# A two-branch encoder on one core: the prompt's squares summed once, more junk products at the start, sample rows in three loads, keys transposed later

## The chip, the cores and the metric

The kernel runs on one core of a Trainium2 chip. Such a core has several engines with queues of their own, each of which works its instructions off in order: TensorE (PE in the profile; PEld are its weight loads), VectorE (DVE), ScalarE (ACT), GpSimd (POOL) and SyncE (SP), which issues nearly all the DMA transfers here. They wait for each other by semaphores. The metric is the device time of one execution in microseconds (us), the median of several runs.

## The reference

Two layers over two groups of tokens, a prompt of 512 and a sample of 256, with 1024 features. In each layer the input is normalised by its root mean square, scaled and shifted by a modulation made from a condition vector, and projected; branch A is neighbourhood attention with 8 heads, branch B grouped-query attention with 8 query and 2 key heads, whose queries and keys are normalised per head and rotated.

```python
mod = jax.nn.silu(c) @ w_ada + b_ada
shift, scale, gate = jnp.split(mod, 3, axis=-1)
hid = _rms_norm(x, norm_g) * (1.0 + scale[:, None, :]) + shift[:, None, :]
proj = hid @ w_in
...
oa = _neighbourhood_attention(qa, ka, va, rpb)
ya = (oa * jax.nn.silu(za)) @ w_pa
qh = _axial_rope(_rms_norm(qb, q_norm_g))
kh = _axial_rope(_rms_norm(kb, k_norm_g))
ob = _gqa_attention(qh, kh, vb)
yb = (ob * jax.nn.silu(zb)) @ w_pb
merged = g_a * ya + g_b * yb
return x + gate[:, None, :] * (merged @ w_out)
```

(Reshapes are left out in these lines; g_a and g_b are sigmoid gates of the input.) After the two layers comes a last normalisation.

## The kernel before

**Tiles.** Activations lie with features on partitions: eight tiles per group, 128 x 512 for the prompt (`xs[0][k]`) and 128 x 256 for the sample (`xs[1][k]`; three of them share one tile in memory, `x_s`). Every operand of a projection is split into a high part and a remainder: ACT copies the high part (`whi` of the weights, `hh` of the activations, `zh`, `GK`), DVE subtracts to get the remainder (`wlo`, `hl`, `zl`), and a product takes three matmuls, high x high, high x low and low x high. In the profile the first projection is `accw<-whi,hh` and so on (512 columns), and later ones are `accp` (512 columns, the prompt) and `accs` (256 columns, the sample).

**Start.** Before the first accw stand, on TensorE: *junk* products of constants (`warm`); the modulation of the first layer, `adap` (the condition with one quarter of `wad`, four matmuls for two loads `adaraw`) and `adat` (its rows turned into columns); the sum of the prompt's squares over the features, `ssps`, by products with ones; and `rb`, which spreads the factor 1/rms over the partitions. ACT squares the eight prompt tiles as they land. `SG="PGPVPGPV"` says for each tile whether its squares are added to those of the tile before, on GpSimd (G) or DVE (V), or begin a new pair (P): four pairs, each summed by an `ssps` set of four products. `ms` and `newton` on DVE (lines 383 and 359 to 366) make the factor. Then DVE scales each x (line 276), ACT makes hh (284), DVE hl (290). The sample goes the same way later, with its seven adds of squares on GpSimd.

The order in this part is made while the program is built: each piece is a `job` with an engine, an assumed duration, what it depends on, and a rank; `run_jobs` plays them through and writes the instructions in the order of the assumed starts. Loads are put in by assumed times of a transfer, and junk products by `WARM=(10, 16.0, 0.8)`: ten at first, then one each 0.8 us of the assumed time until 16. Only the order reaches the chip; there each engine waits for what it needs.

**Later.** From then on the order follows a counter of steps. A `step` writes some six matmuls of a projection, and `defer(n, fn)` puts a piece of other work n steps behind. Attention comes in `slots`, a list that is worked off at a rate of so many per step. Branch B's keys are an example: `kv_evac` takes the key projection from PSUM in three blocks of two token tiles, and rotates it (ACT, DVE, GpSimd); `kfin`, deferred by `KF` steps, makes the per-head factor (the newton chain) and multiplies the rotated keys `rr` by it on DVE (line 1339; of the three blocks the third is deferred by one more step); `ktr`, deferred by `KT` steps, transposes them on TensorE (`kt`, line 1423, four tiles of the prompt and two of the sample), and `evac_k` copies them to `GK` on ACT (lines 676 and 677) and writes their remainders on DVE (680 and 681). All that time the projection of the gate path goes on: ACT takes tanh into `zt`, DVE multiplies (line 1447), GpSimd multiplies by the attention's output (line 1450), ACT copies `zh` (1457), DVE subtracts `zl` (1461). The scores of branch B are `gsp<-GK,GQ`; they use two buffers in PSUM, of which one comes free when ACT has taken the exponential `gp` (line 913), behind the maximum `gss` on DVE (903). `SGQ` is the number of steps before the first scores, and the rate of the slots is `len(slots)/RG`.

Of the kernel before, what the change touches and what calls it, by code (L numbers as in the profile page):

```python
# [7 lines left out]
F32 = mybir.dt.float32  # L8
# [16 lines left out]
SC = dict(  # L25

    LA=7,
    T0=3.6,
    U=0.68,

    SG="PGPVPGPV",
    WARM=(10, 16.0, 0.8),

    PW=("wor01", "wor11", "va3"),

# [6 lines left out]
    QTT=2,  # L42
    QS=6,
    QST=12,
    KF=6,
    KT=8,
    SGQ=12,
    RG=88,

    SR0=90,  # L50
    SR1=40,
# [7 lines left out]


@with_exitstack
def trunk(ctx: ExitStack, tc: tile.TileContext, xT, wst, wad, wsd, vec, gain, trig, mask, eye, rpb, yT):
    nc = tc.nc
    A, V, G, T, S = nc.scalar, nc.vector, nc.gpsimd, nc.tensor, nc.sync

# [49 lines left out]
    def mm(out, lhsT, rhs, start, stop):  # L115
        T.matmul(out=out, lhsT=lhsT, rhs=rhs, start=start, stop=stop, skip_group_check=True)  # L116
# [26 lines left out]
    def defer(k, fn):  # L143
        later.setdefault(step_no[0] + k, []).append(fn)
# [868 lines left out]
    with tc.manual_schedule():  # L1013
# [51 lines left out]

        plan = []

        def load_x(g, k):
            o, n = RNG[g]
            S.dma_start(out=xs[g][k], in_=xT[128 * k:128 * k + 128, o:o + n])  # L1070

        dma = [0.0]

        def load(units, fn):
            t = SC["T0"] + SC["U"] * dma[0]
            dma[0] += units
            plan.append((t - SC["LA"], -1, fn))
            return t + SC["U"] * units
# [58 lines left out]

# [2 lines left out]
        sq = {}  # L1140

        def square(g, k):
            sq[g, k] = galloc([128, RNG[g][1]], F32, "sq")
            A.activation(out=sq[g, k], in_=xs[g][k], func=AF.Square)

        def sq_add(g, k, base, eng):
            eng.tensor_add(out=sq[g, base], in0=sq[g, base], in1=sq[g, k])
            gfree(sq.pop((g, k)))

        def sq_sum(k, first, last):  # L1150
            if first:
                hcell["ps"] = ps_acc.tile([128, 4], F32, tag="acc", name="ssps")
            for i in range(4):
                mm(hcell["ps"][:, i:i + 1], sq[0, k][:, 128 * i:128 * i + 128], ones[:, 0:1],
                   first and i == 0, last and i == 3)
            gfree(sq.pop((0, k)))

        jsum = []
        for k in range(KC):
            j = job("ACT", 0.63, [], lambda k=k: square(0, k), 1, tx[k])  # L1160
            kind = SC["SG"][k]
            if kind in "VG":
                eng, dur = (G, 1.1) if kind == "G" else (V, 0.8)
                j = job("POOL" if kind == "G" else "DVE", dur, [jprev, j], lambda k=k, eng=eng: sq_add(0, k, k - 1, eng), 1)
            jprev, base = j, k - (kind in "VG")
            if k == KC - 1 or SC["SG"][k + 1] == "P":
                jsum.append(job("PE", 0.95, [j] + jsum[-1:],
                                lambda k=base, first=not jsum, last=k == KC - 1: sq_sum(k, first, last), 0))
        j = jsum[-1]
        for (fn,), (eng, dur) in zip(rms_chain(0, hcell)[1:], (("DVE", 2.4), ("PE", 1.0))):  # L1170
            j = job(eng, dur, [j], fn, 0)
        jrb = j
# [19 lines left out]
        for k in range(KC):  # L1192
            j = job("ACT", 0.36, [], lambda k=k: square(1, k), 12, txs[k])
            if k:
                jadd = [job("POOL", 0.6, [j] + jadd, lambda k=k: sq_add(1, k, 0, G), 12)]
            else:
                jadd = [j]

# [2 lines left out]
            sums[0][0]()  # L1201

        sums = rms_chain(1, scell)
        j = job("PE", 0.4, jadd + [jfin[0, 3], jfin[1, 3]], sample_sum, 0)
        for (fn,), (eng, dur) in zip(sums[1:], (("DVE", 2.4), ("PE", 0.5))):
            j = job(eng, dur, [j], fn, 9)
        for k in range(KC):
# [18 lines left out]
        for l in range(DEPTH):  # L1226
# [102 lines left out]
            def rope_finish(rs, ss):  # L1329

                n, nh = ss.shape[1], ss.shape[2]
                V.tensor_scalar(out=ss, in0=ss, scalar1=1.0 / 64, scalar2=EPS, op0=ALU.mult, op1=ALU.add)
                y = newton(ss.rearrange("p t h -> p (t h)"), n * nh).rearrange("p (t h) -> p t h", h=nh)
                t = 0
                for i, r in enumerate(rs):
                    k = r.shape[1]

                    def scale(r=r, k=k, t=t):
                        V.tensor_mul(out=r, in0=r, in1=y[:, t:t + k, :].unsqueeze(3).to_broadcast([128, k, nh, 64]))

                    t += k
                    if i < 2:
                        scale()
                    else:
                        defer(i // 2, scale)
# [6 lines left out]
            def q_evac(i, acc):  # L1352
                qr[i] = galloc([128, 1, 8, 64], F32, "rr")
                rope_part(acc.rearrange("p (t h d) -> p t h d", t=1, d=64), tabs[0][:, i:i + 1], qr[i], qss[:, i:i + 1, :])
                if i == 3:
                    defer(SC["QF"], lambda: rope_finish([qr[t] for t in range(4)], qss[:, 0:4, :]))
                    for pr in range(4):
                        defer(SC["QT"] + SC["QTT"] * pr, lambda pr=pr: q_tr_p(pr))
                if i == 5:
                    defer(SC["QS"], lambda: rope_finish([qr[t] for t in (4, 5)], qss[:, 4:6, :]))  # L1360
                    for w in range(2):
                        defer(SC["QST"] + SC["QTT"] * w, lambda w=w: q_tr_s(w))
# [28 lines left out]
            wide_pass(("qb", l), [(0, 1), (2,), (3,), (4, 5)], q_evac,  # L1391
                      lambda i: ps_acc.tile([128, NP], F32, tag="acc", name="accw"))
            nxt(("kvb", l))
            kr = []
            kss = smp.tile([128, 6, 2], F32, tag="qss2", name="qss", bufs=1)
            vg = vp.tile([128, 6, 4, 128], F32R, tag="v", name="vg")

            def kv_evac(b, acc):
                kr.append(galloc([128, 2, 2, 64], F32, "rr"))
                rope_part(acc[:, :, 0:128].rearrange("p t (h d) -> p t h d", d=64), tabs[1][:, 2 * b:2 * b + 2], kr[b],  # L1400
                          kss[:, 2 * b:2 * b + 2, :])
# [10 lines left out]
            roping[0] = False  # L1412

            def kfin():
                rope_finish(kr, kss)

            def ktr():
                o = [r[:, t].rearrange("p h d -> p (h d)") for r in kr for t in range(2)]
                GK.extend([[galloc([128, NT], F32R, "GK") for _ in range(2)] for _ in range(2)])
                for g, (c, n) in enumerate(RNG):  # L1420
                    t = ps_t.tile([128, n], F32, tag="t", name="kt")
                    for j in range(n // 128):
                        T.transpose(t[:, 128 * j:128 * j + 128], o[4 * g + j], ident)
                    for hp in range(2):
                        evac_k(GK[hp][0], GK[hp][1], hp, t, slice(c, c + n))
                for t_ in kr:
                    gfree(t_)
                for t_ in tabs:
                    gfree(t_)

            defer(SC["KF"], kfin)
            defer(SC["KT"], ktr)
# [268 lines left out]
def _layout(inputs):  # L1701
# [100 lines left out]
    rp = np.zeros((DEPTH, 8, RPB_LEN), dtype=f)  # L1802
    rp[:, :, 820 - 464:820 + 1] = flat[:, :, ::-1]

    arrays = dict(xT=xT, wst=wst, wad=wad, wsd=wsd, vec=vec, gain=gain, trig=trig, mask=mask, eye=np.eye(128, dtype=f), rpb=rp)
    return {k: np.ascontiguousarray(v) for k, v in arrays.items()}


_INS = ["xT", "wst", "wad", "wsd", "vec", "gain", "trig", "mask", "eye", "rpb"]


# [22 lines left out]
```

## Time and profile before

| | us |
|---|---|
| median of 3 runs | 1252.98 |
| lowest and highest | 1250.73, 1256.64 |
| profiled execution | 1254.29 |
| its span | 1252.5 |
| TensorE busy in it | 1216.3 (97%) |
| VectorE, ScalarE, GpSimd busy | 813.2, 580.9, 358.3 |
| mean granted TensorE clock | 0.984 of full |

A timeline row has the start, the time taken, engine, line, operation, output and inputs with their shapes, a count, and in brackets the idle time of the engine before it with what ended that. A matmul's own time includes its tail, so the cost of one in a dense row is the distance between two starts. In a row of the windows view the numbers are the stretch, its length, and for each engine its busy time and its instructions, then the granted clock, the DMA share and GB/s.

### The profile page before, as it was taken

The numbers are of one execution on the slowest core, as the hardware profiler recorded it, in microseconds if no ns is written. First come the engines' busy times: TensorE is split into PE (matmuls) and PEld (weight loads), VectorE is DVE, ScalarE is ACT, GpSimd is POOL, SyncE is SP. The second block draws the span as 40 slices with busy tenths as digits, with TensorE's granted clock in tenths as the row PEclk, the third lists the DMA queues.
The fourth block names the chain that finished last, engine by engine and source line by source line (L and its number), as shares of the span: only waits on it lengthen the run. The fifth ranks groups of instructions, "written<-read, shape, count | busy, mean of one in ns | idle before, by whom it ended". The sixth has DMA issues, their size and how long they took to land.

```text
span 1252.5 us, 19508 instructions
## 1 busy us (share of the span) xinstructions
PE 1216.3 (97%) x7283; PEld 1065.0 (85%) x7283; DVE 813.2 (65%) x1600; ACT 580.9 (46%) x1229; POOL 358.3 (29%) x391
## 2 busy tenths in 40 slices
PE   9999999899999999999999999998999999999997
PEld 6689988798988988887888998887989998878887
DVE  3657887865556447998384678777555545683435
ACT  3347765555555432333153676554555543232323
POOL 0214445433222121111041352644322222221102
PEclk6999999999999999999999999999999999999999
DMA  9433231210111125556462333112011012332334
GB/s 323 160 107 90 79 101 35 66 36 18 51 51 52 51 81 155 177 169 186 141 174 82 95 88 98 59 37 66 20 52 51 20 49 90 123 108 68 109 111 151
DMA packets 48845, 118.28 MB, mean 94 GB/s; under 512 B 5488, under 2 KB 13040, under 8 KB 48752
## 3 DMA queue, kind: packets, MB, share of 16 engines
q1 hardware_dynamic: 48608, 116.98, 30.4%
q8 instruction: 57, 0.93, 0.3%
q14 instruction: 36, 0.29, 0.1%
q10 hardware_dynamic: 144, 0.07, 0.0%
HBM read 110.74 MB, written 6.29 MB: 93 GB/s over the span
## 4 chain that ended last, share of the span: by engine, by line
PE 78%; DVE 12%; ACT 4%; issue 3%; DMA 1%; POOL 1%; SPq 0%; DVEq 0%; POOLq 0%; ACTq 0%
PE accp L116 35%; PE accs L116 17%; PE accw L116 8%; PE go L116 3%; PE gsp L116 3%; PE gtp L938 3%; PE acct L116 3%; DVE adaacc L446 3%; DVE wlo L229 2%; ACT p L776 1%; PE sp L116 1%; PE adap L116 1%; PE op L116 1%; DVE ptl L705 1%; ACT whi L223 1%
## 5 line engine op out<-in xcount | busy, mean ns | idle before, releaser
L116 PE MATMUL accp<-hh,whi 128*128 128x512 f32 x512 | 203.2, 397 | 0.0
L116 PE MATMUL accp<-hh,wlo 128*128 128x512 f32 x512 | 200.2, 391 | 2.1 <-DVE wlo L229 2.1
L116 PE MATMUL accp<-hl,whi 128*128 128x512 f32 x512 | 200.2, 391 | 0.0
L229 DVE TENSOR_TENSOR wlo<-raw,whi 128x1024 fp32r<-128x1024 f32 x119 | 157.4, 1323 | 14.7 <-ACT whi L223 14.3
L927 POOL TENSOR_TENSOR gp<-gp,gss 128x512 f32<-128x512 f32 x80 | 86.6, 1083 | 213.3 <-DVE gss L925 175.4
L116 PE MATMUL accs<-hh,whi 128*128 128x256 f32 x512 | 147.5, 288 | 0.0
L116 PE MATMUL accs<-hl,whi 128*128 128x256 f32 x512 | 146.0, 285 | 0.0
L116 PE MATMUL accs<-hh,wlo 128*128 128x256 f32 x512 | 146.0, 285 | 0.0
L223 ACT ACTIVATE whi<-raw 128x1024 fp32r<-128x1024 f32 x124 | 130.0, 1052 | 18.0 <-PE accw L116 9.8
L116 PEld LDWEIGHTS accp<-hh,wlo 128*128 128x128 f32 x512 | 96.1, 188 | 24.5 <-DVE wlo L229 3.8
L116 PEld LDWEIGHTS accp<-hh,whi 128*128 128x128 f32 x512 | 96.3, 188 | 17.5
L116 PEld LDWEIGHTS accp<-hl,whi 128*128 128x128 f32 x512 | 96.4, 188 | 17.2
L116 PEld LDWEIGHTS accs<-hl,whi 128*128 128x128 f32 x512 | 99.5, 194 | 1.4
L116 PEld LDWEIGHTS accs<-hh,whi 128*128 128x128 f32 x512 | 99.4, 194 | 1.3
L116 PEld LDWEIGHTS accs<-hh,wlo 128*128 128x128 f32 x512 | 99.3, 194 | 0.0
L700 ACT ACTIVATE pth<-gtp 128x512 fp32r<-128x512 f32 x80 | 47.7, 597 | 97.9 <-PE go L116 74.6
L1546 POOL TENSOR_TENSOR th<-th 128x512 f32<-128x512 f32 (+1 forms) x32 | 43.5, 1369 | 171.1 <-DVE th L1539 171.1
L446 DVE SCALAR_TENSOR_TENSOR adaacc<-adaraw,csil,adaacc 128x512 f32<-128x512 f32 x112 | 86.6, 828 | 3.6 <-DMA adaraw<-in_wsd 3.5
L705 DVE TENSOR_TENSOR ptl<-gtp,pth 128x512 fp32r<-128x512 f32 x80 | 54.6, 685 | 47.3 <-ACT pth L700 47.2
L116 PE MATMUL accw<-whi,hh 128*128 128x512 f32 x192 | 78.2, 407 | 0.0
L903 DVE TENSOR_REDUCE gss<-gsp 128x1 f32<-128x512 f32 x64 | 43.9, 687 | 51.4 <-PE gsp L116 51.1
L116 PE MATMUL accw<-wlo,hh 128*128 128x512 f32 x192 | 75.7, 394 | 0.0
(245 smaller groups left out, 2978.6 us busy)
## 6 DMA issues: line engine op xcount, KB each, us to landing
raw<-in_wst SPq DMA_DIRECT2D x124, 512.0 KB, 3.6
adaraw<-in_wsd SPq DMA_DIRECT2D x64, 256.0 KB, 3.3
adaraw<-in_wad SPq DMA_DIRECT2D x32, 256.0 KB, 5.9
u<-in_rpb SPq DMA_DIRECT2D x16, 354.5 KB, 5.2
u<-in_rpb SPq DMA_DIRECT2D x16, 236.5 KB, 4.6
out_y<-y SPq DMA_DIRECT2D x12, 256.0 KB, 2.5
x<-in_xT SPq DMA_DIRECT2D x8, 256.0 KB, 5.3
res<-in_xT SPq DMA_DIRECT2D x8, 256.0 KB, 3.3
```

Of the source, the lines that this page charges most:

```text
L116: T.matmul(out=out, lhsT=lhsT, rhs=rhs, start=start, stop=stop, skip_group_check=True)
L223: A.activation(out=hi, in_=r, func=AF.Copy)
L229: eng.tensor_sub(out=lo, in0=r, in1=hi.bitcast(F32))
L446: V.scalar_tensor_tensor(out=acc[n, h, g], in0=r, scalar=c, in1=acc[n, h, g], op0=ALU.mult, op1=ALU.add)
L700: A.activation(out=h, in_=t, func=AF.Copy)
L705: V.tensor_sub(out=lo, in0=t, in1=h.bitcast(F32))
L776: A.activation(out=P[:, j, :], in_=P[:, j, :], func=AF.Exp, scale=-1.0, bias=ss[:, j:j + 1], accum_out=ss[:, 2 + j:3 + j])
L903: V.tensor_reduce(out=ss[:, 0:1], in_=sp, axis=AX.X, op=ALU.max, negate=True)
L927: G.tensor_mul(out=pv_, in0=pv_, in1=ss[:, 4:4 + n].unsqueeze(2).to_broadcast([128, n, w]))
L938: T.transpose(t[:, q, 128 * j:128 * j + 128], src, ident)
L1546: G.tensor_add(out=t[:, sl], in0=t[:, sl], in1=mrg[k][:, sl])
```

## The change

1. The prompt's squares: `SG` is gone. GpSimd adds the squares of tiles 2 and 3; DVE adds, into tile 0, those of 1, 4, (2+3), 5, 6 and 7; one `ssps` set sums the result.
2. `WARM` is (18, 18.0, 0.45): eighteen junk products at first, then one each 0.45 us of assumed time until 18.
3. The sample's rows come in three loads (three, three and two tiles) from an input `xq` that holds them side by side, in place of eight. Their squares are added on DVE, and the product that sums them also depends on the eleventh of the sixteen steps of the first projection.
4. The keys: `KF` 6 to 7, `KT` 8 to 13, `SGQ` 12 to 16, `RG` 88 to 84. The three blocks of rotated keys are one tile, multiplied by their factor in two pieces, of four and two token tiles, with none deferred. The queries' cosine table is given back earlier.

```diff
-    SG="PGPVPGPV",
-    WARM=(10, 16.0, 0.8),
+    WARM=(18, 18.0, 0.45),
...
-    KF=6,
-    KT=8,
-    SGQ=12,
-    RG=88,
+    KF=7,
+    KT=13,
+    SGQ=16,
+    RG=84,
...
             if i == 3:
-                txs = [load(0.5, lambda k=k: load_x(1, k)) for k in range(KC)]
+                for j in range(3):
+                    w = min(3, KC - 3 * j)
+                    t = load(w / 2, lambda j=j, w=w: S.dma_start(out=x_s[j][:, 0:w, :], in_=xq[:, 3 * j:3 * j + w, :]))
+                    txs += [t] * w
...
+        js = [job("ACT", 0.63, [], lambda k=k: square(0, k), 1, tx[k]) for k in range(KC)]
+        jg = job("POOL", 1.2, [js[2], js[3]], lambda: sq_add(0, 3, 2, G), 1)
+        j = js[0]
+        for k, d in ((1, js[1]), (4, js[4]), (2, jg), (5, js[5]), (6, js[6]), (7, js[7])):
+            j = job("DVE", 0.75, [j, d], lambda k=k: sq_add(0, k, 0, V), 1)
+        j = job("PE", 0.95, [j], sq_sum, 0)
+        jsum = [j]
...
-                jadd = [job("POOL", 0.6, [j] + jadd, lambda k=k: sq_add(1, k, 0, G), 12)]
+                jadd = [job("DVE", 0.45, [j] + jadd, lambda k=k: sq_add(1, k, 0, V), 12)]
...
-        j = job("PE", 0.4, jadd + [jfin[0, 3], jfin[1, 3]], sample_sum, 0)
+        j = job("PE", 0.4, jadd + [jfin[0, 3], jfin[1, 3], jva[-6]], sample_sum, 0)
...
                 if i == 5:
+                    defer(3, lambda: gfree(tabs[0]))
...
-            kr = []
+            kr = galloc([128, 6, 2, 64], F32, "rr")
...
-                rope_finish(kr, kss)
+                rope_finish([kr[:, 0:4], kr[:, 4:6]], kss)
```

**The order on TensorE at the start.** Before, its first rows are these:

```order
L116 MATMUL junk<-cst 128x512 x12
L116 MATMUL ssps<-ones,sq 128x1 x4
L116 MATMUL junk<-cst 128x512 x2
L116 MATMUL ssps<-ones,sq 128x1 x4
L116 MATMUL junk<-cst 128x512 x2
L116 MATMUL ssps<-ones,sq 128x1 x4
L116 MATMUL junk<-cst 128x512
L116 MATMUL adap<-adaraw,c_104 32x256 x4
L116 MATMUL ssps<-ones,sq 128x1 x4
L116 MATMUL junk<-cst 128x512 x2
```

Then come three groups of four adap, two pairs of adat and rb, with five junk products between them, eight adap, and the first accw: in all 22 junk, 24 adap. With the change the first rows are these:

```order
L115 MATMUL junk<-cst 128x512 x29
L115 MATMUL adap<-adaraw,c_104 32x256 x4
L115 MATMUL junk<-cst 128x512 x3
L115 MATMUL adap<-adaraw,c_104 32x256 x4
L115 MATMUL junk<-cst 128x512 x2
L115 MATMUL ssps<-ones,sq 128x1 x4
L115 MATMUL junk<-cst 128x512 x2
L115 MATMUL adat<-sel,rows 128x2 x2
L115 MATMUL junk<-cst 128x512
L115 MATMUL adap<-adaraw,c_104 32x256 x4
L115 MATMUL junk<-cst 128x512
L115 MATMUL adap<-adaraw,c_104 32x256 x4
```

and these, up to the first accw:

```order
L115 MATMUL junk<-cst 128x512 x4
L115 MATMUL rb<-ident,ny 128x128 x4
L115 MATMUL junk<-cst 128x512 x2
L115 MATMUL adat<-sel,rows 128x2 x2
L115 MATMUL junk<-cst 128x512
L115 MATMUL adap<-adaraw,c_104 32x256 x4
L115 MATMUL junk<-cst 128x512
L115 MATMUL adap<-adaraw,c_104 32x256 x4
L115 MATMUL adat<-sel,rows 128x2 x2
L115 MATMUL adap<-adaraw,c_104 32x256 x8
L115 MATMUL accw<-whi,hh_343 128x512
```

That is 46 junk and 32 adap products (eight groups of four), one ssps set and three adat pairs ahead of the first accw.

**The order around the keys.** On DVE, before, from the end of the newton chain on:

```order
L366 SCALAR_TENSOR_TENSOR ny<-na,ny 128x12
L1339 TENSOR_TENSOR rr<-rr,ny 128x256 x2
L1447 SCALAR_TENSOR_TENSOR zt<-zt,accp 128x512
L229 TENSOR_TENSOR wlo<-raw,whi 128x1024
L1339 TENSOR_TENSOR rr<-rr,ny 128x256
L680 TENSOR_TENSOR GK<-kt,GK 64x512
L681 TENSOR_TENSOR GK<-kt,GK 64x512
```

and with the change:

```order
L365 SCALAR_TENSOR_TENSOR ny<-na,ny 128x12
L1333 TENSOR_TENSOR rr<-rr,ny 128x512
L1333 TENSOR_TENSOR rr<-rr,ny 128x256
L1454 TENSOR_TENSOR zl<-zt,zh 128x512
L1440 SCALAR_TENSOR_TENSOR zt<-zt,accp 128x512
L1454 TENSOR_TENSOR zl<-zt,zh 128x512
L679 TENSOR_TENSOR GK<-kt,GK 64x512
L680 TENSOR_TENSOR GK<-kt,GK 64x512
```

The first gate product and a wlo have moved ahead of the newton chain, and two zl stand ahead of the key remainders. On ACT the eight copies to GK come first before the change (four of the prompt, four of the sample), then zh; with the change they stand behind a zh and a zt, and behind them come:

```order
L676 ACTIVATE GK<-kt 64x256
L1450 ACTIVATE zh<-zt 128x512
L1437 ACTIVATE zt<-accs 128x256 x2
L222 ACTIVATE whi<-raw 128x1024
L1450 ACTIVATE zh<-zt 128x256 x2
L1437 ACTIVATE zt<-accp 128x512
L222 ACTIVATE whi<-raw 128x1024
L912 ACTIVATE gp,gss<-gsp,gss 128x512 x2
```

The second zl on DVE takes the zh that stands behind the copies. On TensorE kt came, before, behind the last accp of a chunk and ahead of its 48 accs, and the first gsp behind these; with the change those 48 accs and six accp of the next chunk come first, then kt, 18 accp, two gsp, 12 accp, two gsp, six accp, two gsp.

More of the change, by code (lines that the diff above doesn't have):

```diff
@@ L61, in trunk @@
 @with_exitstack
-def trunk(ctx: ExitStack, tc: tile.TileContext, xT, wst, wad, wsd, vec, gain, trig, mask, eye, rpb, yT):
+def trunk(ctx: ExitStack, tc: tile.TileContext, xT, xq, wst, wad, wsd, vec, gain, trig, mask, eye, rpb, yT):
     nc = tc.nc
@@ L1066, in trunk, with load_x @@
         plan = []
-        def load_x(g, k):
-            o, n = RNG[g]
-            S.dma_start(out=xs[g][k], in_=xT[128 * k:128 * k + 128, o:o + n])
+        def load_x(k):
+            S.dma_start(out=xs[0][k], in_=xT[128 * k:128 * k + 128, 0:NP])
         dma = [0.0]
@@ L1127, in trunk @@
         tu = {}
-        tx = [load(1, lambda k=k: load_x(0, k)) for k in range(KC)]
+        tx = [load(1, lambda k=k: load_x(k)) for k in range(KC)]
         txs = []
@@ L1148, in sq_add, with sq_sum @@
             gfree(sq.pop((g, k)))
-        def sq_sum(k, first, last):
-            if first:
-                hcell["ps"] = ps_acc.tile([128, 4], F32, tag="acc", name="ssps")
+        def sq_sum():
+            hcell["ps"] = ps_acc.tile([128, 4], F32, tag="acc", name="ssps")
             for i in range(4):
[L1154 to L1169, printed above, removed]
+                mm(hcell["ps"][:, i:i + 1], sq[0, 0][:, 128 * i:128 * i + 128], ones[:, 0:1], i == 0, i == 3)
+            gfree(sq.pop((0, 0)))
+        js = [job("ACT", 0.63, [], lambda k=k: square(0, k), 1, tx[k]) for k in range(KC)]
[5 more added lines that the diff above has]
+        jsum = [j]
         for (fn,), (eng, dur) in zip(rms_chain(0, hcell)[1:], (("DVE", 2.4), ("PE", 1.0))):
@@ L1398, in kv_evac @@
             def kv_evac(b, acc):
-                kr.append(galloc([128, 2, 2, 64], F32, "rr"))
-                rope_part(acc[:, :, 0:128].rearrange("p t (h d) -> p t h d", d=64), tabs[1][:, 2 * b:2 * b + 2], kr[b],
+                rope_part(acc[:, :, 0:128].rearrange("p t (h d) -> p t h d", d=64), tabs[1][:, 2 * b:2 * b + 2],
+                          kr[:, 2 * b:2 * b + 2],
                           kss[:, 2 * b:2 * b + 2, :])
@@ L1414, in kfin @@
             def kfin():
-                rope_finish(kr, kss)
+                rope_finish([kr[:, 0:4], kr[:, 4:6]], kss)
             def ktr():
-                o = [r[:, t].rearrange("p h d -> p (h d)") for r in kr for t in range(2)]
+                o = [kr[:, t].rearrange("p h d -> p (h d)") for t in range(6)]
                 GK.extend([[galloc([128, NT], F32R, "GK") for _ in range(2)] for _ in range(2)])
@@ L1425, in ktr @@
                         evac_k(GK[hp][0], GK[hp][1], hp, t, slice(c, c + n))
[L1426 to L1429, printed above, removed]
+                gfree(kr)
+                gfree(tabs[1])
             defer(SC["KF"], kfin)
@@ L1803, in _layout @@
     rp[:, :, 820 - 464:820 + 1] = flat[:, :, ::-1]
-    arrays = dict(xT=xT, wst=wst, wad=wad, wsd=wsd, vec=vec, gain=gain, trig=trig, mask=mask, eye=np.eye(128, dtype=f), rpb=rp)
+    xq = xT[:, NP:].reshape(KC, 128, NS).transpose(1, 0, 2)
+    arrays = dict(xT=xT, xq=xq, wst=wst, wad=wad, wsd=wsd, vec=vec, gain=gain, trig=trig, mask=mask, eye=np.eye(128, dtype=f), rpb=rp)
     return {k: np.ascontiguousarray(v) for k, v in arrays.items()}
-_INS = ["xT", "wst", "wad", "wsd", "vec", "gain", "trig", "mask", "eye", "rpb"]
+_INS = ["xT", "xq", "wst", "wad", "wsd", "vec", "gain", "trig", "mask", "eye", "rpb"]
 def kernel(**inputs):
```

## The prediction

> **What bounds the kernel now.** I read the page first, then the waits of TensorE, then its timeline at the start and around the key transposes, with the windows view for the granted clock.
>
> ```profile
> span 1252.5 us, 19508 instructions
> PE kt L1423 <- DVE rr L1339: 10.7, 4, 2.9
> ```
>
> The profiled execution took 1254.29 us, 1.8 more than its span; the three runs have a median of 1252.98. The second row heads the list of TensorE's waits (total, times, longest): kt, 10.7 us in the two layers. TensorE sets the end: in the rows below it is idle only where a wait stands. What is not in that list is the clock:
>
> ```profile
> 10.00:20.00 10.00, 10.00 (x48) 6.66 (x52) 2.66 (x13) 1.54 (x3) 1.21 (x1) 0.50 1.05 394
> 20.00:30.00 10.00, 10.00 (x56) 6.28 (x57) 3.69 (x7) 2.65 (x5) 0.00 (x0) 0.56 0.89 314
> 50.00:60.00 10.00, 8.12 (x33) 6.37 (x32) 4.88 (x16) 1.41 (x3) 2.13 (x3) 0.83 0.17 52
> ```
>
> Each row: the stretch, its length, busy time of PE, PEld, DVE, ACT, POOL, the granted clock, then DMA share and GB/s. From 10 to 20 us TensorE is busy all the time and yet at half clock. Its list of small products (squares, modulation, junk) is itself the path to the first layer product, and at 0.50 that list takes twice as long as it need. The row from 50 to 60 us has 10 x 0.17 / 0.5 = 3.4 us at half clock, behind the sample's wait.
>
> **The start, up to the first accw.** These are TensorE's rows before the first layer product; start-to-start distances give the cost of each kind, at half clock above 28.86 and at full clock below.
>
> ```profile
> 1.19 4.73 PE L116 MATMUL junk<-cst 128*128 128x512 f32 x12 [1.19 <-DVE cst L1017]
> 15.30 1.87 PE L116 MATMUL ssps<-ones,sq 128*128 128x1 f32 x8
> 23.93 2.08 PE L116 MATMUL rb<-ident,ny 128*128 128x128 f32 x8
> 25.66 0.77 PE L116 MATMUL junk<-cst 128*128 128x512 f32 x1
> 26.23 0.85 PE L116 MATMUL adat<-sel,rows 128*128 128x2 f32 x4
> 27.01 1.92 PE L116 MATMUL adap<-adaraw,c 128*32 128x256 f32 x16
> 28.86 0.50 PE L116 MATMUL accw<-whi,hh 128*128 128x512 f32 x1
> 30.37 0.50 PE L116 MATMUL adat<-sel,rows 128*128 128x2 f32 x4
> 30.80 0.64 PE L116 MATMUL adap<-adaraw,c 128*32 128x256 f32 x8
> 31.37 0.50 PE L116 MATMUL accw<-whi,hh 128*128 128x512 f32 x1
> ```
>
> At half clock: rb 1.73 us, a junk product 0.57, an adat pair 0.78, a group of four adap products (x8 in the rows) 0.93, a set of four ssps 1.87. At full clock: adat 0.43, an adap group 0.57; rb, ssps and junk by halves 0.87, 0.93 and 0.29.
>
> The change takes three of the four ssps sets away (5.6 us at half clock), raises the junk before the first accw from 22 products to 46, and puts 32 adap products there in place of 24. The squares' sum becomes one chain on DVE:
>
> ```profile
> 7.89 3.33 ACT L1144 ACTIVATE sq<-x 128x512 f32<-128x512 f32 x5 [1.31 <-DMA x<-in_xT]
> 11.24 0.69 DVE L1147 TENSOR_TENSOR sq<-sq 128x512 f32<-128x512 f32 x1 [2.00 <-ACT sq L1144]
> 17.21 0.16 DVE L383 TENSOR_SCALAR ms<-ssps 128x4 f32<-128x4 f32 x1 [5.28 <-PE ssps L116]
> 19.39 0.17 DVE L366 SCALAR_TENSOR_TENSOR ny<-na,ny 128x4 f32<-128x4 f32 x1
> 11.93 5.74 SPq L1084 DMA_DIRECT2D adaraw<-in_wad  x8
> adaraw<-in_wad SPq DMA_DIRECT2D x32, 256.0 KB, 5.9
> ```
>
> The loads of x stay, so ACT's last square ends at 11.22 as before; five of the six DVE adds (0.69 each) fit between the squares, and the last ends near 12.0. The newton chain takes 19.56 - 17.21 = 2.35 us. Now TensorE's list after the change. 29 junk products stand first. The row of 12 took 0.39 each. If the first nine go at that rate and the other 20 at the full rate of 0.23 (accp rows below), they end at 9.3; if all go at 0.39, at 12.5. I take 9.7, nearer the first: of 0.39, between 0.23 and 0.57, a part must have been at the full rate already. Behind it stand eight adap groups, three adat pairs, rb, one ssps set and 17 junk products.
>
> At full clock that is 8 x 0.57 + 3 x 0.43 + 0.87 + 0.93 + 17 x 0.29 = 12.6 us, so 22.3. Neither the sum (ssps is reached at about 12.2) nor the newton chain (done near 15.7, rb reached at 16.7) is late then. The last adap group needs the sixteenth adaraw, issued by 17.67 and landed 5.9 later, at 23.6; with its product 24.2. **I take the first accw at 24.0, 4.9 us sooner than 28.86.** At half clock the list is 8 x 0.93 + 3 x 0.78 + 1.73 + 1.87 + 17 x 0.57 = 23.1 us: first accw at 32.8, 3.9 us later than now. So the clock decides the sign, and the rows do not show it for this list: a list of mixed products at half clock did not win the clock back for some 18 us, but in the change 8 us of dense junk come first, and the clock has only to be kept. I take full clock, because of the dense block, with the other end as a rival.
>
> [...]
>
> **The sample's sum.** Seven adds leave GpSimd for DVE, three loads take the place of eight, and the product of the sum moves from behind the ninth accw step to behind the eleventh.
>
> ```profile
> 52.34 0.73 PE L116 MATMUL ssps<-ones,sq 128*128 128x1 f32 x4 [1.88 <-POOL sq L1147]
> 45.31 6.98 POOL L1147 TENSOR_TENSOR sq<-sq 128x256 f32<-128x256 f32 x7 [34.11 <-DMA raw<-in_wst]
> 32.64 5.71 SPq L1070 DMA_DIRECT2D x0s<-in_xT  x8
> 253.27 0.43 DVE L681 TENSOR_TENSOR GK<-kt,GK 64x256 fp32r<-64x256 f32 x1
> ```
>
> GpSimd's seven adds take 6.98 us; on DVE, by the nearest row of 256 elements, 7 x 0.43 = 3.0, and DVE was busy 4.88 of the 10 us around. That removes the wait of 1.88 and, if nothing else idles there, the 3.4 us at half clock (1.7 us lost). In TensorE's queue the product then stands 12 accw before its rb, not 18: 12 x 0.23 = 2.8 us of cover against 0.59 for ssps, 2.35 for the newton chain and gaps of some 0.3, so a new wait of 0.4 to 0.8; and a late square could leave up to 1.9 as now. I take 0.8. The shorter SP stretch (three issues of 0.71 against 5.71) lets the next weights start some 3.6 us sooner; nothing waits for them there, so nothing is credited. Two adap groups have moved ahead of the first accw: 1.1 us less behind it.
>
> Start in all: 4.9 + 1.9 + 1.7 + 1.1 - 0.8 = **8.8 us less**; at half clock 3.9 - 3.9 = 0.
>
> **The keys.** The transposes kt move five steps down TensorE's queue, the rotary finish one step.
>
> ```profile
> 245.78 0.69 PE L1423 MATMUL kt<-ident,rr 128*128 128x128 f32 x4 [2.46 <-DVE rr L1339]
> 249.38 0.66 PE L1423 MATMUL kt<-ident,rr 128*128 128x128 f32 x2 [2.91 <-DVE rr L1339]
> 254.09 0.28 PE L116 MATMUL accs<-hh,wlo 128*128 128x256 f32 x1
> 257.44 0.63 PE L116 MATMUL gsp<-GK,GQ 128*128 128x512 f32 x2
> 257.90 0.39 PE L116 MATMUL accp<-hh,whi 128*128 128x512 f32 x1
> 260.64 0.61 PE L116 MATMUL gsp<-GK,GQ 128*128 128x512 f32 x2
> 248.00:254.00 6.00, 4.62 (x22) 4.66 (x23) 5.86 (x10) 3.53 (x8) 0.94 (x1) 0.50 0.27 87
> 850.00:860.00 10.00, 5.14 (x32) 4.89 (x33) 9.52 (x21) 4.99 (x10) 2.11 (x1) 0.83 0.17 52
> 245.21 0.76 DVE L1339 TENSOR_TENSOR rr<-rr,ny 128x256 f32<-128x256 f32 x2
> 247.75 1.48 DVE L1339 TENSOR_TENSOR rr<-rr,ny 128x256 f32<-128x256 f32 x1
> 246.84 2.11 POOL L1450 TENSOR_TENSOR zt<-zt,oa 128x512 f32<-128x512 f32 x1 [4.02 <-DVE zt L1447]
> ```
>
> In each layer kt waits 2.46 + 2.91 = 5.37 us (10.7 in all), and TensorE goes on at half clock: 4.7 us of it after 249.38 in the first layer, some 2.7 in the second (10 x 0.17 / 0.5 = 3.4, part of it waiting), with 0.44 of that lost: 2.0 and 1.2. Between 254.09 and 257.44 stand 28 accs, 0.12 each; between 257.90 and 260.64 12 accp, 0.23 each. The 48 accs and 6 accp that now stand ahead of kt are 5.8 + 1.4 = 7.2 us, so TensorE arrives at 243.3 + 7.2 = 250.5. On DVE a gate product (0.69) and a weight remainder (1.22) now come before the newton chain, so the factor is there at 245.1 + 1.9 = 247.0, and both rr pieces by 248.2. Were they stretched as the row of 1.48 is, beside a GpSimd product that took 2.11, it would be 250.5: at worst just in time. The wait goes: 10.7 + 3.2 = 13.9 us.
>
> [...]
>
> What is late next? Between kt and the first gsp stood 48 accs; now there stand 18 accp.
>
> ```profile
> 246.51 0.59 ACT L676 ACTIVATE GK<-kt 64x512 fp32r<-64x512 f32 x1 [5.88 <-PE kt L1423]
> 250.07 0.38 ACT L676 ACTIVATE GK<-kt 64x256 fp32r<-64x256 f32 x1 [1.16 <-PE kt L1423]
> 251.52 0.62 ACT L1457 ACTIVATE zh<-zt 128x512 fp32r<-128x512 f32 x1
> 249.15 0.68 DVE L680 TENSOR_TENSOR GK<-kt,GK 64x512 fp32r<-64x512 f32 x1
> ```
>
> From kt's start: ACT begins the copies 0.73 later, four of 0.60 and four of 0.39 (3.96), then zh 0.62: 5.3. On DVE a remainder zl (0.69) stands ahead of the key remainders and needs that zh: 6.0; two key remainders of 0.68 end at 7.4. TensorE needs them for the second product of the first gsp, at 0.9 + 18 x 0.23 = 5.0, and 0.2 behind the first: **a wait of 2.2 us per layer**. Further on, the third gsp needs the buffer that ACT's gp of the first gives back. TensorE reaches it at 7.4 + 0.5 + 2.7 + 0.5 + 1.4 = 12.5. ACT's gp stands behind zh copies that need GpSimd's zt, which need DVE's products behind all eight key remainders (6.0 + 4 x 0.69 + 4 x 0.43 = 10.5, products to 11.2, GpSimd to about 12.7, ACT's zh, zt, whi and gp to 15.5): a wait of 2 to 4, I take 3. In the kernel before, no wait for gp stands in the list. Both per layer: 10.4 us given back. A wait of 1.88 brought the clock down for 3.4 us in the row from 50 to 60, so these may too: 1.5 us each time, none to four times; I take one.
>
> [...]
>
> Keys in all: 13.9 - 10.4 - 1.5 = **2.0 us less**, between 4.5 more (waits of 2.2 and 4, four falls) and 13.9 less. Total 8.8 + 2.0 = 10.8: 1254.29 - 10.8 = 1243.5 for an execution like the profiled one, 1242.2 against the median. **I predict 1242.**
>
> **Rivals.**
> *The start falls to half clock.* For it: 20 us at 0.50 to 0.56 with TensorE busy; against it: the dense block ahead. From the first mixed product on it gives 0 at the start and 2.0 at the keys, 1251; from half-way through the list, 3 to 5 us of gain, 1247. I price it at 1249.5.
> *The keys give nothing back.* If the gsp operands come in time, because ACT or DVE run ahead of my chain, 8.8 + 13.9 = 22.7: 1230 against the median. Against it: the order of ACT and DVE, which is fixed.
> *kt still waits.* If rr is late again, the 13.9 stay and no gsp waits: 1253 - 8.8 = 1244. Margin 2.3 us, or none with the stretched pieces.
> *Slower: the clock goes against every piece.* [...] The start loses 3.9 and a further 1.5 of accw at half clock, against 3.9 saved; at the keys four falls of 1.5 and gsp waits of 2.2 and 4 (12.4) against 13.9. That is 1.5 + 4.5 = 6 more: 1259. [...]
>
> **How the numbers follow.** Forecast 0.50 (1242, its own range 1237 to 1248), half clock at the start 0.25, keys in full 0.14, kt late 0.04, slower 0.07. Half a per cent is 6.3 us, about what a measurement here can tell from no change; 1246.7 and 1259.2 are the borders. Faster: 0.43 of the forecast's half, 0.05 of the second, 0.14 and 0.03: 0.65. Slower: half of the slow rival and bits of the second and of the forecast, 0.07. The rest, 0.28, is no change. The range reaches into the full gain and up to the half-clock start: 1235 to 1252.
>
> **What would show it.** In the profile of the changed kernel: granted clock 1.00 from 10 to 24 us and the first accw near 24; one ssps set near 12.5 without a wait; no ssps wait for the sample; the last accw of the first projection some 8 to 9 us sooner; no kt row in the waits, and in its place gsp waiting for GK remainders (about 2.2, twice) and for gp (2 to 4, twice). I am wrong if the clock is at 0.50 from 10 to 25 us, or if gsp does not stand in the waits at all.

## The result and the profile after

The changed kernel takes 1244.65 us (median of 5 runs, 1244.16 to 1247.67) against 1252.98 (median of 5 runs, 1250.72 to 1256.64). The ratio is 0.9939 with a 95% interval of 0.9915 to 0.9963: 0.6% faster, 8.3 us by the medians. The execution that was profiled took 1244.36 us with a span of 1242.6, 9.9 less than the span before.

The page's first row and the waits of TensorE in the changed kernel (total, times, longest):

```profile
span 1242.6 us, 19501 instructions
PE gsp L115 <- ACT gp L912: 5.6, 2, 3.6
PE op L115 <- DVE ptl L704: 5.2, 4, 1.6
PE gsp L115 <- DVE GK L680: 4.1, 2, 2.0
PE rb L115 <- DVE ny L365: 3.1, 2, 1.7
PE adap L115 <- DMA adaraw<-in_wad: 1.4, 1, 1.4
```

The row that headed the list before, kt with 10.7, is gone, and two gsp rows with 9.7 together have come. There is no row for ssps behind the sample's squares. The wait of adap for its load is new.

The windows view at the start and around the keys of both layers; the last three numbers of a row are the granted clock, the DMA share and GB/s:

```profile
10.00:20.00 10.00, 8.96 (x66) 5.64 (x67) 5.55 (x20) 2.54 (x5) 0.00 (x0) 1.00 1.05 391
20.00:30.00 10.00, 9.41 (x74) 5.96 (x73) 7.45 (x14) 4.28 (x7) 0.00 (x0) 1.00 1.04 391
50.00:60.00 10.00, 10.00 (x48) 8.31 (x47) 7.70 (x25) 4.88 (x14) 0.00 (x0) 1.00 0.01 2
250.00:260.00 10.00, 6.40 (x24) 4.84 (x23) 8.65 (x15) 4.15 (x9) 4.88 (x5) 0.86 0.27 67
850.00:860.00 10.00, 7.97 (x28) 6.13 (x27) 7.64 (x13) 4.16 (x10) 2.10 (x2) 0.83 0.01 2
```

Where the clock stood at 0.50 and 0.56 before, it is 1.00 now, although TensorE is less busy (8.96 and 9.41 in place of 10.00): it waits 1.4 us for a load and 0.6 for ACT's rows of the modulation, and runs the rest about twice as fast (by the distance of the starts, rb takes 0.81 us against 1.73 and a set of ssps 0.81 against 1.74). The stretch from 50 to 60 us is full and at full clock. Around the keys one stretch at half clock is left in each layer (0.86 and 0.83; in shorter stretches of the view 0.50 from 258 to 260 and from 855 to 857 us).

TensorE's timeline of the changed kernel, at the places that the prediction named:

```profile
1.19 8.41 PE L115 MATMUL junk<-cst 128*128 128x512 f32 x29 [1.19 <-DVE cst L1016]
11.04 1.22 PE L115 MATMUL adap<-adaraw,c 128*32 128x256 f32 x8 [1.43 <-DMA adaraw<-in_wad]
14.22 0.95 PE L115 MATMUL ssps<-ones,sq 128*128 128x1 f32 x8
18.95 1.05 PE L115 MATMUL rb<-ident,ny 128*128 128x128 f32 x8
23.30 0.61 PE L115 MATMUL adat<-sel,rows 128*128 128x2 f32 x4 [0.59 <-ACT rows L413]
24.84 0.50 PE L115 MATMUL accw<-whi,hh 128*128 128x512 f32 x1
48.56 0.50 PE L115 MATMUL ssps<-ones,sq 128*128 128x1 f32 x4
51.78 0.61 PE L115 MATMUL rb<-ident,ny 128*128 128x128 f32 x4
65.86 0.39 PE L115 MATMUL accp<-hh,whi 128*128 128x512 f32 x1
240.74 0.82 PE L1418 MATMUL kt<-ident,rr 128*128 128x128 f32 x6
245.53 0.39 PE L115 MATMUL gsp<-GK,GQ 128*128 128x512 f32 x1
247.94 0.50 PE L115 MATMUL gsp<-GK,GQ 128*128 128x512 f32 x1 [2.03 <-DVE GK L680]
251.03 0.61 PE L115 MATMUL gsp<-GK,GQ 128*128 128x512 f32 x2
256.60 0.80 PE L115 MATMUL gsp<-GK,GQ 128*128 128x512 f32 x2 [3.60 <-ACT gp L912]
854.25 0.64 PE L115 MATMUL gsp<-GK,GQ 128*128 128x512 f32 x1 [2.03 <-DVE GK L680]
862.92 0.73 PE L115 MATMUL gsp<-GK,GQ 128*128 128x512 f32 x2 [2.04 <-ACT gp L912]
```

The first accp, the first product behind the first projection, stood here before:

```profile
75.44 0.39 PE L116 MATMUL accp<-hh,whi 128*128 128x512 f32 x1
```

It comes 9.6 us sooner, so in these two executions nearly the whole difference of the spans arises at the start. The six kt run without a wait, the first gsp is halted before its second product, and the third gsp waits for the buffer of the first. The two layers do not wait alike for gp: in the second, seven of the 12 accp ahead of it ran at half clock (0.43 us from start to start against 0.23), TensorE came later, and the wait is 1.6 us shorter.

### The profile page after: what moved, and what is told of

The parts are those of the page before. It is cut to its first block, busy times and chain, and to the rows that moved or that the text cites. A ratio compares the mean times of both kernels' runs of the same rounds, so it can differ in the third digit from the quotient of the medians.

```text
span 1242.6 us, 19501 instructions
## 1 busy us (share of the span) xinstructions
PE 1208.7 (97%) x7282; PEld 1058.6 (85%) x7282; DVE 818.4 (66%) x1609; ACT 580.6 (47%) x1229; POOL 347.6 (28%) x383
## 4 chain that ended last, share of the span: by engine, by line
PE 78%; DVE 11%; ACT 5%; issue 3%; DMA 1%; POOL 1%; SPq 0%; DVEq 0%; ACTq 0%; POOLq 0%
PE accp L115 35%; PE accs L115 17%; PE accw L115 8%; PE go L115 3%; PE gsp L115 3%; PE gtp L937 3%; PE acct L115 3%; DVE adaacc L445 3%; DVE wlo L228 2%; ACT p L775 1%; PE sp L115 1%; PE op L115 1%; ACT whi L222 1%; PE adap L115 1%; DVE ptl L704 1%
## 5 line engine op out<-in xcount | busy, mean ns | idle before, releaser
L926 POOL TENSOR_TENSOR gp<-gp,gss 128x512 f32<-128x512 f32 x80 | 83.4, 1042 | 213.8 <-DVE gss L924 192.5
L722 POOL TENSOR_TENSOR bm<-u,masks 128x128 f32<-128x128 f32 (+2 forms) x80 | 41.3, 539 | 152.4 <-DMA u<-in_rpb 152.4
```

Of the source, the lines that this page charges most:

```text
L722: G.tensor_tensor(out=o.rearrange("p (c r) -> p c r", r=r), in0=u, in1=mk.rearrange("p (c r) -> p c r", r=r), op=ALU.add)
L926: G.tensor_mul(out=pv_, in0=pv_, in1=ss[:, 4:4 + n].unsqueeze(2).to_broadcast([128, n, w]))
```

## The experiments

The experiments were measured in later sessions than the changed kernel, and the kernel before was measured again in each: its medians there are 1253.41 (e1 to e4), 1254.57 (e5 to e7 and e10) and 1253.99 (e11 and e12), against 1252.98. Ratios are to the kernel before in the same session. Where a time is set against the changed kernel's 1244.65, a difference of a microsecond or so can come from the session.

**Each part alone.** Two kernels divide the change into its start (parts 1 to 3) and its keys (part 4).

```diff
 e1_start_only, against the changed kernel
-    KF=7,
-    KT=13,
-    SGQ=16,
-    RG=84,
+    KF=6,
+    KT=8,
+    SGQ=12,
+    RG=88,
...
-            kr = galloc([128, 6, 2, 64], F32, "rr")
+            kr = []
...
```

> The changed kernel with its keys put back as they were (KF, KT, SGQ, RG, the three blocks of rotated keys), so parts 1 to 3 of the change alone. My reading of the changed kernel's trace: the start has brought 9.6 us (first accp 65.86 against 75.44) and the keys next to nothing (waits of kt 10.7 and some 3 at half clock gone, gsp waits of 9.7 in their place and a piece at half clock). So 1253 - 9.6 = 1243.5, within 2 us of the changed kernel, with kt waiting 10.7 us as before. Rival, the keys carry a good part of the gain (the 13.9 less what really came back): 1247 or more.

Measured: 1246.44 us (1246.04 to 1247.44, 5 runs), ratio to the kernel before 0.9945 (0.9929 to 0.9961). The start alone brings 7.0 of the 8.8 us that the changed kernel has against the same shared median of 1253.41; 1.8 us above the changed kernel, at the outer edge of the theory's 2 us and 0.6 below the rival. TensorE's waits in this kernel begin with

```profile
PE kt L1417 <- DVE rr L1333: 10.7, 4, 2.9
```

and its first accp is at 65.86, exactly as in the changed kernel. By the medians the keys' old order therefore costs 1.8 us and not nothing, but the runs of the two kernels overlap (1246.04 to 1247.44 and 1244.16 to 1247.67), so it is not clear of noise. My "next to nothing" came from comparing the profiled executions of before and after, and the one of before had met a short stretch at half clock behind the second layer's kt (0.83 from 850 to 860 us, 3.4 us). Here, in the windows view of the start-only kernel, it is 5.6 + 1.2 = 6.8 us, one stretch more:

```profile
840.00:850.00 10.00, 4.79 (x24) 4.54 (x25) 9.49 (x21) 4.99 (x10) 2.11 (x1) 0.72 0.17 53
850.00:860.00 10.00, 10.00 (x58) 9.00 (x58) 5.53 (x10) 4.20 (x10) 3.72 (x4) 0.94 0.01 2
```

The second kernel is the one before with part 4 alone.

```diff
 e2_keys_only, against the kernel before
-    KF=6,
-    KT=8,
-    SGQ=12,
-    RG=88,
+    KF=7,
+    KT=13,
+    SGQ=16,
+    RG=84,
...
-                rope_finish(kr, kss)
+                rope_finish([kr[:, 0:4], kr[:, 4:6]], kss)
```

> The kernel before with part 4 of the change alone. Theory: kt's wait goes, gsp waits of about 2 (key remainders) and 2 to 4 (gp) per layer stand in its place: 1253 - 0.5, within 2 us of before; first accw at 28 to 29 and half clock from 10 to 28 us as before. The prediction's own sum said 2.0 less, 1251. Rival, the keys gain when the start does not disturb them: 1247 or less.

Measured: 1251.13 us (12 runs), ratio 0.9988 (0.9973 to 1.0003): 2.3 us by the medians, not clear of nothing. Its waits of TensorE show the exchange undisturbed by the start:

```profile
PE gsp L116 <- DVE GK L681: 4.1, 2, 2.0
PE gsp L116 <- ACT gp L913: 4.0, 2, 2.0
```

So kt's 10.7 went and 8.1 came back. With the first kernel this gives 7.0 + 2.3 = 9.3 us for the parts against 8.8 for the whole: they add, as far as the scatter lets one say.

**What in the start brings it.** The prediction rested on the junk: a dense block first, then full clock. Two kernels exchange only that, one from each side.

```diff
 e3_junk_only, against the kernel before
-    WARM=(10, 16.0, 0.8),
+    WARM=(18, 18.0, 0.45),
 e4_old_junk, against the changed kernel
-    WARM=(18, 18.0, 0.45),
+    WARM=(10, 16.0, 0.8),
```

> The kernel before with only WARM changed to (18, 18.0, 0.45): the four ssps sets stay. Theory (a dense block of junk at first keeps the clock): granted clock near 1.00 from 10 to 25 us, first accw at 22 to 24.5, the sample's wait of 1.9 and its stretch at half clock still there or somewhat larger: 1246 to 1249. Rival (the four sets of squares and the waits between them are what lost the clock): half clock from about 8 us on, and 24 more junk products at 0.57 on the path: first accw at 33 or later, 1257 or more.

Measured: 1249.65 us (10 runs, 1247.52 to 1253.47), ratio 0.9976 (0.9961 to 0.9991). In the profiled execution the clock stayed up with all four ssps sets in the list, as the theory said, and the first accw came at 23.52; the rival's half clock from 8 us on did not show:

```profile
10.00:20.00 10.00, 10.00 (x78) 6.64 (x78) 2.98 (x15) 1.78 (x4) 0.41 (x1) 1.00 1.05 392
46.49 0.60 PE L116 MATMUL ssps<-ones,sq 128*128 128x1 f32 x4 [1.37 <-POOL sq L1147]
```

The gain is 3 to 4 us, less than the 4 to 7 expected, and the execution that was profiled (1247.79) is among its faster ones. The sample's wait stayed, as it should.

> The changed kernel with WARM back at (10, 16.0, 0.8), so the squares summed once but the old junk. Theory: the junk block ends near 7.5 us, adap waits for its load until 11.0 as in the changed kernel, the clock falls behind 3.5 us of idling, and the list runs at half clock: first accw near 28 to 29 against 24.8, in all 4 to 5.5 us more than the changed kernel, 1249. Rival (one ssps set in place of four is what brings the gain): first accw at 25 or sooner, 1245 or less.

Measured: 1244.28 us (4 runs, 1243.85 to 1247.64), ratio 0.9932 (0.9912 to 0.9952): no slower than the changed kernel. The theory, 1249, is out. The execution that was profiled is the slowest of the four (1247.64, mean clock 0.991; the other three have 0.994), and it shows what the theory described, only cheaper:

```profile
10.00:20.00 10.00, 9.22 (x45) 5.08 (x49) 4.75 (x18) 1.01 (x2) 0.00 (x0) 0.60 1.05 393
20.00:30.00 10.00, 9.41 (x81) 6.45 (x73) 6.78 (x12) 4.69 (x8) 0.00 (x0) 0.89 1.04 391
10.78 1.20 PE L115 MATMUL adap<-adaraw,c 128*32 128x256 f32 x8 [3.56 <-DMA adaraw<-in_wad]
26.23 0.50 PE L115 MATMUL accw<-whi,hh 128*128 128x512 f32 x1
```

TensorE waits 3.56 us for the load, the clock goes to half (0.50 from 14 to 22 us), and yet the first accw comes only 1.4 us later than in the changed kernel, since there is less junk to carry along and the clock is back by some 22 us. I had priced the fall without the shorter list. So new junk on the old sums brings 3 to 4 us, and the rest of the change with the old junk brings as much as the whole. That rest is the new sums, the sample's part and the keys together; no run has the new sums alone. Taking the sample's 2.0 (below) and the keys' 1.8 off its 9.1 leaves some 5 us for the new sums, an estimate from differences that are each near the scatter.

Two more kernels take away the junk between the other products:

```diff
 e11_block_only, against the changed kernel
-    WARM=(18, 18.0, 0.45),
+    WARM=(29, 0.0, 0.45),
 e12_short_block_only, against the changed kernel
-    WARM=(18, 18.0, 0.45),
+    WARM=(17, 0.0, 0.45),
```

> The changed kernel with all 29 junk products of its first block and none of the 17 between the other products. Theory (the block brings the clock up, the junk between keeps it): TensorE now waits for loads between the adap groups, the clock falls to half at about 12 to 15 us, comes back as the accw run; the list is 17 x 0.29 = 4.9 us shorter but the loads set the pace: first accw at 24 to 26, in all 0 to 2 us above the changed kernel. Rival (the junk between is only in the way): clock 1.00 throughout, first accw at 23.5 or sooner, 1 us or more below the changed kernel.

Measured: 1244.05 us (5 runs, 1241.44 to 1246.48), ratio 0.9921 (0.9895 to 0.9947).

> The same with a block of 17 and none between. Theory (the clock is down from 12 us on anyway, as in the run with the old junk, and what counts is the length of the list at half clock against the loads): half clock from about 12 to 22 us or later; list without its 7 junk products 4 us shorter, so first accw by the loads at 23.5 to 25.5, in all within 2 us of the changed kernel. [...]

Measured: 1244.27 us (4 runs, 1243.89 to 1245.00), ratio 0.9925 (0.9900 to 0.9949). Both equal the changed kernel within their scatter. But their profiled executions differ in a way that neither expectation had. The long block alone, then the short one alone, from 10 to 30 us, with the first accw of each:

```profile
10.00:20.00 10.00, 8.89 (x67) 5.67 (x69) 6.54 (x21) 2.41 (x4) 0.00 (x0) 0.84 1.05 394
20.00:30.00 10.00, 9.41 (x61) 5.55 (x54) 6.61 (x12) 4.27 (x7) 0.00 (x0) 0.65 1.04 391
24.73 0.80 PE L115 MATMUL accw<-whi,hh 128*128 128x512 f32 x1
```

```profile
10.51 2.55 PE L115 MATMUL adap<-adaraw,c 128*32 128x256 f32 x16 [3.10 <-DMA adaraw<-in_wad]
10.00:20.00 10.00, 8.36 (x72) 4.42 (x72) 6.89 (x22) 2.28 (x5) 0.00 (x0) 1.00 1.05 394
22.39 0.50 PE L115 MATMUL accw<-whi,hh 128*128 128x512 f32 x1
```

With 29 products of junk ahead and no wait above 1 us behind them the clock fell, at about 17 us (0.50 from 18 to 26 us); with 17 ahead and a wait of 3.10 us it stayed at 1.00. Within one kernel the runs differ as well (the long block alone: mean clocks from 0.991 to 0.995, times from 1241.44 to 1246.48 us). So the length of the dense block alone does not decide the clock of this stretch. What does is not settled by these runs.

What holds for the changed kernel and its three variants of junk is the time: 1244.05 to 1244.65. The first accw moves between 22.39 and 26.23 in their profiled executions, but not all of it reaches the end. The row of the short block alone, whose first accw is 2.4 us and whose first accp 1.6 us sooner than in the changed kernel:

```profile
PE gsp L115 <- ACT gp L912: 7.2, 2, 3.6
```

It waits 3.6 for gp in both layers, 1.6 more than the changed kernel, which came to the second of these waits later, after products at half clock (0.50 from 855 to 857 us).

**The sample's part.**

```diff
 e10_sample_old, against the changed kernel
-                for j in range(3):
-                    w = min(3, KC - 3 * j)
-                    t = load(w / 2, lambda j=j, w=w: S.dma_start(out=x_s[j][:, 0:w, :], in_=xq[:, 3 * j:3 * j + w, :]))
-                    txs += [t] * w
+                txs = [load(0.5, lambda k=k: S.dma_start(out=xs[1][k], in_=xT[128 * k:128 * k + 128, NP:NT])) for k in range(KC)]
...
-                jadd = [job("DVE", 0.45, [j] + jadd, lambda k=k: sq_add(1, k, 0, V), 12)]
+                jadd = [job("POOL", 0.6, [j] + jadd, lambda k=k: sq_add(1, k, 0, G), 12)]
...
-        j = job("PE", 0.4, jadd + [jfin[0, 3], jfin[1, 3], jva[-6]], sample_sum, 0)
+        j = job("PE", 0.4, jadd + [jfin[0, 3], jfin[1, 3]], sample_sum, 0)
```

> The changed kernel with part 3 undone: eight loads of the sample's rows, their squares added on GpSimd, the sum's product free to stand sooner (it stands three steps sooner in the order). Theory (the sample's part is worth its old wait and the half clock behind it): TensorE reaches the product near 44.4, GpSimd's seven adds of 1.0 end near 46 to 47, a wait of 2 to 3 and perhaps 1.7 at half clock, against a wait of 0.8 for rb less: 2 to 4 us above the changed kernel, 1247 to 1249. Rival (the start alone brings the gain, the sum would be in time on GpSimd too): within 1 us of the changed kernel.

Measured: 1246.66 us (6 runs, 1244.19 to 1249.52), 2.0 above the changed kernel by the medians, at the lower edge of the theory, with scatter that reaches the rival. In the execution that was profiled, its slowest, the wait is back:

```profile
45.82 0.60 PE L115 MATMUL ssps<-ones,sq 128*128 128x1 f32 x4 [1.56 <-POOL sq L1145]
68.87 0.39 PE L115 MATMUL accp<-hh,whi 128*128 128x512 f32 x1
```

It costs 3.0 us up to the first accp there, the wait and the stretch at half clock behind it (accw 0.43 us from start to start, from 47.38 to 50.37, against 0.23).

**Where the keys' gain went, and how to keep it.** If the gsp waits are the price, then an order without them should be worth nearly all of it. Two edits of numbers try that, alone and together.

```diff
 e5_keys_one_step_sooner, against the changed kernel
-    KT=13,
+    KT=12,
 e6_late_scores, against the changed kernel
-    SGQ=16,
-    RG=84,
+    SGQ=28,
+    RG=72,
 e7_both: these two edits together
```

> The changed kernel with KT 12 in place of 13: the eight key remainders then stand on DVE ahead of the zl that waits for the zh behind ACT's key copies, all else as it is. Theory (that zl is what makes the first gsp wait, and through DVE's gate products and GpSimd also the third): the gsp wait for GK (2 x 2.0) goes, and the wait for gp (3.6 and 2.0) falls to 0 to 1 each, with a stretch at half clock less: 6 to 10 us below the changed kernel, 1235 to 1239. Rival (gp waits for ACT's own queue, not for that chain): only the 4.1 go, 1240.5. Second rival (kt comes too soon for rr again): a kt wait of 1 us or more per layer, 1243 or more.

Measured: 1237.86 us (5 runs, 1237.19 to 1241.51), ratio 0.9881 (0.9856 to 0.9906), 6.8 below the changed kernel. The key remainders now stand on DVE ahead of the zl that waits for zh, and the wait for GK is gone from the list. The zl and the second key remainder on DVE in the first layer of the changed kernel, and that remainder in this one:

```profile
245.91 0.69 DVE L1454 TENSOR_TENSOR zl<-zt,zh 128x512 fp32r<-128x512 f32 x1 [5.60 <-ACT zh L1450]
247.21 0.68 DVE L680 TENSOR_TENSOR GK<-kt,GK 64x512 fp32r<-64x512 f32 x1
```

```profile
242.57 0.69 DVE L680 TENSOR_TENSOR GK<-kt,GK 64x512 fp32r<-64x512 f32 x1
```

TensorE's timeline of the first layer in this kernel:

```profile
238.79 0.82 PE L1418 MATMUL kt<-ident,rr 128*128 128x128 f32 x6
244.93 0.62 PE L115 MATMUL gsp<-GK,GQ 128*128 128x512 f32 x2
248.11 0.62 PE L115 MATMUL gsp<-GK,GQ 128*128 128x512 f32 x2
252.70 0.73 PE L115 MATMUL gsp<-GK,GQ 128*128 128x512 f32 x2 [2.62 <-ACT gp L912]
```

The first row has no wait: kt is not too soon. The edit does two things at once: it changes DVE's order, and it puts kt six accp further ahead of the first gsp. Counted from kt's start, the second remainder ends at 7.15 in the changed kernel and at 4.47 here; TensorE reached the product that needs it at 5.17 there and reaches it near 6.4 here. By these rows the order alone would have been enough (4.47 against 5.17), and the distance alone would have left some 0.8 of the wait (7.15 against 6.4); both are estimates, since no run parts the two.

The wait for gp fell less than expected, to 2.6 per layer and not to 0 to 1; 5.2 in all against 5.6. ACT's gp still stands behind two zh copies that wait for GpSimd's zt (2.88 and 1.26 us of idle time on ACT in the first layer, 4.87 and 1.24 in the changed kernel), and DVE's gate products for them still stand behind all eight key remainders. The time is the theory's all the same: of the 6.5 us between the spans of the profiled executions 4.5 are waits of gsp and 0.6 the start (first accp at 65.29), and the first layer's stretch at half clock is gone (1.00 from 250 to 260 us); the second layer's is still there (0.83 from 850 to 860 us).

> The changed kernel with SGQ 28 in place of 16 and RG 72 in place of 84: the scores begin twelve steps later and are written at a higher rate, so that they end at the same step. Theory (the gsp waits are the price of beginning too soon): no gsp row in the waits, 9.7 us and one or two stretches at half clock (1.5 each) gone: 1232 to 1235. Rival (at 1.61 slots a step in place of 1.38, DVE, ACT and GpSimd cannot keep up, and the waits come back in gtp or go): less than 4 us gained, 1241 or more.

Measured: 1232.71 us (4 runs, 1231.82 to 1232.93), ratio 0.9832 (0.9810 to 0.9854), 11.9 below the changed kernel. There is no gsp row in its waits, and the higher rate of the scores costs nothing that shows.

> Both edits: KT 12, SGQ 28, RG 72. Theory: the two remove the same waits, so they do not add: within 1.5 us of the later scores alone, 1231 to 1234. Rival, each removes waits that the other leaves: 1229 or less.

Measured: 1230.77 us (4 runs, 1229.49 to 1231.47), ratio 0.9816 (0.9794 to 0.9839), 13.9 below the changed kernel and 1.9 below the late scores alone, a little more than the theory allowed. The late scores alone have a small new wait, which the second edit takes away: the rival's mechanism, at a smaller size than it said; the row of the late scores and then the stretches of both edits around the keys:

```profile
PE accs L115 <- DVE zt L1440: 1.5, 2, 0.8
```

```profile
250.00:260.00 10.00, 10.00 (x69) 9.24 (x68) 7.20 (x10) 5.42 (x10) 3.97 (x5) 1.00 0.31 105
850.00:860.00 10.00, 10.00 (x65) 9.12 (x64) 6.66 (x8) 4.48 (x9) 5.01 (x4) 1.00 0.28 90
```

In these stretches TensorE is busy 10.00 of 10 us at full clock in both layers. This version is faster than both kernels of the change, by 1.1% than the one and 1.8% than the other.

## Why the prediction was right, and where it was not

The forecast was 1242, range 1235 to 1252; measured 1244.65. The likeliest case came about, with both halves as they were forecast (full clock at the start, one set of waits exchanged for another at the keys), and it was 2.4 us too fast by the medians; the sum's 10.8 us stand against 8.3 by the medians and 9.9 by the two profiled executions.

*The start, 8.8 forecast, 9.6 in the profiled executions.* The first accw came at 24.84 and not at 24.0: 4.0 us gained and not 4.9. The list did run at full clock (1.00 from 10 to 30 us), but adap waited until 11.04 for its first loads and the last adat 0.59 for ACT, two waits that the sum did not have, and the list itself took 13.2 us from there, where I had 12.6. The bound that gave the 24.0, the sixteenth adaraw landing at 23.6, did not come into play: the last adap products stood at 23.84 with no idle time before them, and with the short block alone the first accw came at 22.39, behind all eight groups. So 24.0 was near 24.84 in part by luck, a load priced too late in place of waits left out. The squares' chain was also late, five of its DVE adds running from 8.87 to 13.28 and not to near 12.0; ssps stood at 14.22 behind the wait of adap and so did not feel it. Two readings were a little off without moving the forecast: a set of ssps costs 1.74 at half clock by the distance of the starts (15.30 to 17.04), 1.87 being its own time, and by the prices given rb stands at 17.1 and not 16.7.

From the first accw to the first accp the time fell from 46.6 to 41.0, 5.6 us, where I had 3.9: the new wait of rb for the newton chain, 0.8, did not come (no bracket in the row at 51.78, the chain was just hidden behind the 12 accw), and an adat pair of 0.4 that also moved ahead of the first accw was counted in the list there but not credited behind it. That makes 5.1; the other 0.5 is not followed up. Alone and by medians the start is worth 7.0.

*The reason given for it fell in part.* "I take full clock, because of the dense block" was the step on which the sign hung. The clock was at 1.00, but the runs with other junk show that the block of 29 is not what the time hangs on: with a block of 17, with the old junk, or with none between, the changed sums take 1244 us all the same. No run is without a block. That the sign came out right is therefore no proof of this reason; what decides the clock there stays open. And a fall of the clock need not cost what the end at half clock, "first accw at 32.8", assumed: where it did fall, the first accw came at 26.23 with the old junk and 24.73 with none between. Those lists are shorter, and half clock did not last for the whole of them: with the old junk it was over by some 22 us, with none between it began at about 17 and was over by some 27. With the new junk a fall did not occur in a profiled execution, so 32.8 itself was not tried.

*The keys, 2.0 forecast, 1.8 and 2.3 by the two kernels that part the change, neither clear of noise by itself.* The wait of kt went. The wait for GK was to be 2.2 per layer and is 2.03; the wait for gp was to be 3, between 2 and 4, and is 3.60 and 2.04. The chain through ACT's key copies, zh, DVE's zl and the key remainders stands in the rows of the changed kernel (zl waits for zh until 245.91, the second remainder ends at 247.89, gsp starts at 247.94), and with the remainders ahead of that zl and kt one step sooner the GK wait disappears. One stretch at half clock was assumed in all and there is one per layer; the one ahead of the second layer's gp wait cost little: seven accp at 0.43 us in place of 0.23 are 1.4 us, and the wait behind them was 1.6 shorter than in the first layer.

*The rivals.* "The keys give nothing back", 1230, was what the change could have had: the two edits reach 1230.77, with all its steps in place. The split is another than in that rival, though: against the start-only kernel it is 15.7 for the keys, beside 7.0 for the start, where the rival had 13.9 and 8.8. "kt still waits" is excluded by its row. "Slower" did not come about.

## What to carry to other kernels

A transpose that waits for its operand can be moved down the queue, but then its consumers must be moved too: here five steps for the transposes with four for the scores exchanged 10.7 us of waiting for 9.7, and twelve steps more for the scores took those 9.7 away. Before moving a piece, walk the chain behind it on the slower engines, in their order, up to the first instruction of the bounding engine that needs it, and look for an instruction in that chain that waits for something unrelated (here one zl). And when a list of small products runs at a low granted clock (0.50 here), look first whether it can be shortened: here the version with one sum in place of four took the same time whatever the junk was (1244.05 to 1244.65 us), while more junk on the long list brought 3 to 4 us. That the single sum is what did it is argued, since no run has it alone.

## What the runs showed of the hardware

A list of junk and small products that keeps TensorE busy stood at half clock for long (10.00 us busy from 10 to 20 us at 0.50 in the kernel before) and another at full clock with less work in it (8.36 busy at 1.00, after a wait of 3.10 us, with the short block alone). A wait of 2.03 us for GK in the second layer of the changed kernel was followed by half clock (0.50 from 855 to 857 us); behind a wait of the same length in the first layer the clock stayed at 1.00 (from 248 to 253 us). Executions of the kernel before have mean clocks of 0.982 to 0.988 and take 1257 to 1249 us with them, so one profiled execution can lie some 4 us to either side of another's middle. What decides the granted clock is left open by these runs.
